# Three PSUM banks for each pair of a seven-product part, and other places for the weights of 256-column matmuls

## The chip, the cores and the metric

One core of one Trainium2 chip runs the program. The metric is the device time of one execution in microseconds, as the median over runs.

## The reference

A two-layer encoder trunk over 512 tokens of width 1024, in float32. Each layer adds four sub-layers to x: a SwiGLU of hidden width 2816, a mixer (retention and gated DeltaNet heads), a cross-attention to 256 memory rows, and a second SwiGLU. The change touches the SwiGLU most:

```python
def swiglu(u, w_gate, w_up, w_down):
    return (jax.nn.silu(u @ w_gate) * (u @ w_up)) @ w_down
...
for l in range(DEPTH):
    h = swiglu(rms_norm(x, norm_pre[l, 0]), ffn1_gate[l], ffn1_up[l], ffn1_down[l])
    x = x + 0.5 * rms_norm(h, norm_post[l, 0])
...
    h = swiglu(rms_norm(x, norm_pre[l, 3]), ffn2_gate[l], ffn2_up[l], ffn2_down[l])
    x = x + 0.5 * rms_norm(h, norm_post[l, 3])
```

## The kernel before, in words

**Two halves of every number.** TensorE works in a reduced float32. So every operand is held as a high part H and a rest L, and each product takes three matmuls, in this order: weights H with activations H, H with L, L with H (`mm3`, `mm3s`). In the trace such a matmul reads "out<-moving operand,weights". Three of them are called a triple below.

**The stream of weights.** `Stream` brings 1 MB raw tiles by DMA (two buffers, `raw`), and its thread `cutter` (line 431) cuts each into chunks: ScalarE writes H, VectorE writes L = raw - H. Chunks lie in one long tile `wts` (places of 2048 elements; `places`, line 379) or, around a change of sub-layer, in three extra pairs of tiles (`wHx`, `wLx`, made by `hl_tiles` in `transition`, line 817). `where` and `take` choose the place.

**Narrow and wide matmuls.** Most matmuls move 512 columns. 256 columns move in three places: the first group of each sub-layer (`first_group`, line 729, four chunks in two halves of the tokens), the K projection and the scores of the cross-attention, and the seven-product parts.

**Seven-product parts.** In `gate_up` (line 871) the gate and up columns from block `FAST` on are made 256 at a time. One such block of one of the two matrices is called a pair here (two 128-column stripes). It takes seven products of half size in place of eight (a Strassen scheme): each product is four triples, so a pair is 84 matmuls. `forms` (line 887) makes the sums S1 to S4 of the activations, S4 in place of A21; the cutter makes those of the weights, through the tile `T`. The four parts hold 3 + 9 + 9 + 9 blocks, which is 60 pairs and 5040 matmuls. A pair uses two PSUM banks of eight: Y (two partial sums side by side) and X. The order of the products in `stream` (line 961) and the waits between them are

```python
Y1 += c0 * A11;  Y0 += c1 * S1;  X0 += c0' * A12
yield lambda: r["a"]        # Y copied whole, 512 columns
Y0 += c3 * S4;   Y1 += c1' * S2;  X1 += c2 * A22
yield lambda: r["b"]        # Y1 copied, 256 columns
Y1 += c2' * S3
```

`post` (line 919) copies the intermediate sums to an SBUF tile `sg` on ScalarE (three copies), adds what is left in PSUM on VectorE (two of 512 columns), and takes Silu (gate) or multiplies by the gate into `h` (up, two of 512 columns).

**What sets the order.** The program is written out by a list scheduler (`Sched`, line 194): threads yield operations, and per engine the one that can start first by its cost table is emitted, with priorities. Each engine then runs its own queue in that order. `Banks` (line 318) hands out the eight PSUM banks, `Stream.prio` (line 468) sets how eager the cutter is by the number of chunks it is ahead.

**Where operands lie.** The allocator puts `wts` at byte 36,800 of each partition and `uH` at 196,544: 159,744 bytes apart, which is 624 x 256. `uL`, the S tiles and the extra tiles of the transitions behind a SwiGLU or a cross-attention are multiples of 256 away too. So a chunk at a place 2048 i begins at the same place of a 256-byte period as the operand that moves past it. Chunks of the seven-product parts are put 16 elements (64 bytes) on (`SHIFT`, line 366). In `mix` the tiles before the ring `hs` (seven of 128 bytes and one of 64, behind the 16 KB tile `oT`) end 64 bytes short of such a multiple, so the ring, and the extra tiles of the transition opened behind it, begin 64 bytes back.

Of the kernel before, what the change touches and what calls it, by code (L numbers as in the profile page):

```python
# [8 lines left out]
F32R = mybir.dt.float32r  # L9
# [3 lines left out]
ALU = mybir.AluOpType  # L13
AX = mybir.AxisListType

P = 128
D = 1024
S = 512
NT = S // P
KD = D // P  # L20
# [14 lines left out]
LEAD = 3  # L35

# [324 lines left out]
class Stream:  # L361
# [4 lines left out]
    SHIFT = 16  # L366

    def __init__(self, k):
        self.k = k
        self.raws, self.parts, self.loaded, self.chunks = [], [], {}, {}  # L370
        self.cut = self.taken = 0
        self.limit = self.slack = 0
        self.extra = []
        self.T = None

    def open(self, raw, w):
        self.rawring = Ring(raw)
        self.w, self.live = w, set()
        self.places = {"p": [(2048 * i, 1024) for i in range(HL_BUFS)],
                       "s": [(2048 * i + self.SHIFT, 1024) for i in range(HL_BUFS - 1)],  # L380
                       "h": [(2048 * (HL_BUFS - 1) + self.SHIFT, 512)]}

    def add(self, ap, a, b, kind):
# [3 lines left out]
    def cols(self, w, c0, kind="c"):  # L387
        self.add(w[:, c0:c0 + 256].rearrange("(k p) c -> p k c", p=P), KD, 256, kind)
# [18 lines left out]
    def where(self, c):  # L407

        if self.extra and c < self.limit:
            return self.extra  # L410
        i, j = self.parts[c]
        kind = "p" if self.raws[i][3] != "s" else "h" if j == 2 else "s"
        for pl in self.places[kind]:
            if all(pl[0] + 2 * pl[1] <= lo or lo + 2 * n <= pl[0] for lo, n in self.live):
                return kind, pl
        return None

    def take(self, c):
        ch, got = Chunk(), self.where(c)
        if got is self.extra:  # L420
            ch.home, ch.slot = got, got.pop(0)
            return ch, ch.slot
        kind, pl = got
        self.places[kind].remove(pl)
        self.places[kind].append(pl)
# [58 lines left out]
class Kernel:  # L484
# [26 lines left out]
    def hl_tiles(self, pool, i):  # L511
        return tuple(pool.tile([P, 1024], F32R, name=f"w{c}{i}") for c in "HL")

    def plan(self):

        A, st = self.D, self.st
        for l, i in self.subs:
            self.marks.append(len(st.parts))
            if i in (0, 3):
                g, u, d = (A[f"ffn{1 if i == 0 else 2}_{n}"][l] for n in ("gate", "up", "down"))  # L520
                for j in range(0, DFF, 256):
                    kind = "s" if (l, i) in FAST and j >= 256 * FAST[l, i] else "c"
                    st.cols(g, j, kind)
                    st.cols(u, j, kind)
                for k in range(0, DFF, 256):
                    st.rows(d, k)
            elif i == 1:
                w = A["w_in"][l]
                for c in (2560, 2048, 2816, 2304, 3072, 3328):
                    st.cols(w, c)  # L530
# [6 lines left out]
            else:  # L537
                q, k, v = (A[f"xattn_{n}"][l] for n in "qkv")
                for w, c in XORDER:
# [4 lines left out]
                    else:  # L544
                        st.cols(w, c)
# [271 lines left out]
    def transition(self, sub, nxt, stream, half=False, initial=False):  # L817

        n = 0 if initial else self.subs.index(sub) + 1
        with self.pool("trans") as tp:  # L820
# [9 lines left out]
            self.st.extra = [self.hl_tiles(tp, f"x{n}{i}") for i in range(HL_EXTRA)]  # L830
# [40 lines left out]
    def gate_up(self, h, made, ready, last, j0, nxt, hx):  # L871
# [8 lines left out]
        with self.pool("ffs") as fs:  # L880
# [38 lines left out]
            def post(r, j, up):  # L919
                o = yield from sg.get()  # L920
                yield lambda: r["n"] >= 2
                yield self.copy(o[:, 256:768], r["Y"].t)
                r["a"] = True
                yield lambda: r["n"] >= 5
                yield self.copy(o[:, 0:256], r["Y"].t[:, 256:])
                r["b"] = True
                yield lambda: r["n"] >= 7
                yield self.copy(o[:, 768:], r["Y"].t[:, 256:])
                r["c"] = True
                for b, sl in (("Y", slice(0, 512)), ("X", slice(512, 1024))):  # L930
                    yield V.tensor_tensor(out=o[:, sl], in0=r[b].t, in1=o[:, sl], op=ALU.add)
                    r[b].put()
# [6 lines left out]
                for q in (0, 1):  # L939
                    sl = slice(512 - 512 * q, 1024 - 512 * q)  # L940
                    yield self.mul(h[:, 2 * j + q], o[:, sl], g[:, sl])
                    ready.add(2 * j + q)
# [18 lines left out]
            def stream():  # L961
# [12 lines left out]
                for j in range(j0, KF // 2):  # L974
                    for up in range(2):
# [3 lines left out]
                        r = {"n": 0, "a": False, "b": False, "c": False}  # L979
                        r["Y"] = yield from self.banks.get(True)  # L980
                        r["X"] = yield from self.banks.get(True)
                        Y0, Y1 = r["Y"].t[:, :256], r["Y"].t[:, 256:]
                        X0, X1 = r["X"].t[:, :256], r["X"].t[:, 256:]
                        ths.append(sd.spawn(post(r, j, up), lambda r=r: 5 if r["c"] else -1, "post"))
# [12 lines left out]
                        st.free(c1)  # L997
# [3 lines left out]
                        yield lambda: r["b"]  # L1001
                        yield from product(r, Y1, half(c2, 1), S[2], last=True)
# [157 lines left out]
    def mix(self, l, nxt):  # L1160
# [6 lines left out]
        with self.pool("mix") as mp:  # L1167
# [20 lines left out]
            with self.pool("hs") as hp:  # L1188
                self.hring = [tuple(self.tile(hp, f"hs{c}{i}", [S], F32R) for c in "HL") for i in range(6)]
# [731 lines left out]
```

## Time and profile before

| | |
|---|---|
| median of 3 runs | 2445.86 us (2445.59 to 2447.47) |
| the profiled execution's own time | 2445.77 us |
| its span, first to last instruction | 2444.0 us |
| TensorE matmul busy | 2399.7 us (98%) |
| VectorE, ScalarE busy | 1686.7 us (69%), 1122.4 us (46%) |
| mean granted TensorE clock | 0.995 |
| chain that ended last | PE 19%, POOL 1%, the rest under 1% each |

The span is shorter than the time by 1.8 us, which lie before the first and after the last instruction. A matmul's row in a timeline has its start and a duration that overlaps the next one's (matmuls are pipelined); what one costs is the distance from start to start. All instructions stand under line 235, where the scheduler emits them, so groups are told apart by tile names.

### The profile page before, as it was taken

What the parts mean: (1) busy time and instruction counts of PE and PEld (TensorE: products, weight loads), DVE (VectorE), ACT (ScalarE), POOL (GpSimd) and SP (SyncE); (2) the same over time, 40 slices, a digit from 0 to 9 for tenths busy, and PEclk for the clock granted to TensorE, in tenths of its full rate; (3) what the DMA queues carried; (4) which work ended last, traced back from release to release, by engine and by line L of the source; (5) the groups of instructions that cost most, each with busy time, mean ns of one, the idle gap of its engine ahead of it and who ended that gap; (6) DMA issues with size and microseconds to landing.
All of it is one profiled execution on the core that took longest, in us unless ns stands there. A gap on an engine that the chain in (4) does not pass through costs nothing. (4 is left out here: it accounts for less than half of the span.)

```text
span 2444.0 us, 37654 instructions
## 1 busy us (share of the span) xinstructions
PE 2399.7 (98%) x15206; PEld 2128.4 (87%) x15206; DVE 1686.7 (69%) x2660; ACT 1122.4 (46%) x1886; POOL 203.4 (8%) x584
## 2 busy tenths in 40 slices
PE   8999999999999999999999999999999999999998
PEld 7889888886989889998889998888788898899987
DVE  5588637867776568886388885486877665788852
ACT  4524525742345544555245553366324454455631
POOL 1000001221020020001010000114010200100011
PEclk9999999999999999999999999999999999999999
DMA  6622522355334322334213334225553243133330
GB/s 204 202 95 82 177 86 96 99 175 159 99 121 153 109 86 70 114 108 176 86 35 104 106 120 160 81 93 145 163 153 132 89 164 104 35 104 104 127 141 35
DMA packets 231204, 286.83 MB, mean 117 GB/s; under 512 B 29630, under 2 KB 190966, under 8 KB 231030
## 3 DMA queue, kind: packets, MB, share of 16 engines
q1 hardware_dynamic: 229878, 280.23, 35.6%
q10 hardware_dynamic: 1152, 4.19, 0.4%
q8 instruction: 119, 1.95, 0.3%
q14 instruction: 55, 0.45, 0.1%
HBM read 255.00 MB, written 29.39 MB: 116 GB/s over the span
## 5 line engine op out<-in xcount | busy, mean ns | idle before, releaser
L235 PE MATMUL ps<-uH,wts 128*128 128x256 f32 (+1 forms) x4064 | 973.1, 325 | 2.5 <-ACT sg L235 2.0
L235 PEld LDWEIGHTS ps<-uH,wts 128*128 128x128 f32 x4064 | 690.3, 189 | 63.6 <-ACT sg L235 2.2
L235 PE MATMUL ps<-uL,wts 128*128 128x256 f32 (+1 forms) x2032 | 655.9, 323 | 0.6 <-DVE uL L235 0.6
L235 DVE TENSOR_TENSOR wts<-raw,wts 128x1024 fp32r<-128x1024 f32 (+1 forms) x363 | 408.5, 1134 | 141.9 <-ACT wts L235 139.3
L235 ACT ACTIVATE wts<-raw 128x1024 fp32r<-128x1024 f32 (+1 forms) x363 | 354.5, 983 | 202.8 <-PE ps L235 115.4
L235 PEld LDWEIGHTS ps<-uL,wts 128*128 128x128 f32 x2032 | 386.8, 190 | 30.8 <-DVE uL L235 1.5
L235 PE MATMUL ps<-wts,uH 128*128 128x512 f32 x1152 | 356.8, 391 | 0.0
L235 PEld LDWEIGHTS ps<-wts,uH 128*128 128x128 f32 x1152 | 214.9, 188 | 43.6
L235 PE MATMUL ps<-wts,uL 128*128 128x512 f32 x576 | 224.6, 390 | 0.0
L235 ACT ACTIVATE sg<-ps 128x256 f32<-128x256 f32 (+1 forms) x208 | 98.0, 473 | 273.1 <-PE ps L235 272.8
L235 DVE TENSOR_TENSOR wts<-T,wts 128x1024 fp32r<-128x1024 f32 x120 | 147.0, 1225 | 51.3 <-ACT wts L235 50.7
L235 ACT ACTIVATE wts<-T 128x1024 fp32r<-128x1024 f32 x120 | 126.9, 1057 | 62.8 <-DVE T L235 62.8
L235 PEld LDWEIGHTS ps<-wts,uL 128*128 128x128 f32 x576 | 108.2, 188 | 22.8
L235 DVE TENSOR_TENSOR uL<-h,uH 128x512 fp32r<-128x512 f32 x76 | 51.2, 689 | 107.5 <-ACT uH L235 107.4
L235 POOL TENSOR_SCALAR sm<-sm 128x1 f32<-128x1 f32 (+1 forms) x165 | 39.2, 238 | 836.8 <-ACT junk L235 812.1
L235 ACT ACTIVATE uH<-h 128x512 fp32r<-128x512 f32 x76 | 46.3, 626 | 132.0 <-PE ps L235 126.9
L235 ACT ACTIVATE junk<-ps 128x512 bf16<-128x512 f32 (+1 forms) x96 | 47.0, 490 | 113.6 <-PE ps L235 99.2
L235 POOL TENSOR_SCALAR wpost<-wpost 128x1024 f32<-128x1024 f32 x4 | 20.3, 5087 | 925.7 <-DMA wpost<-in_norm_post_dram 701.0
L235 PE MATMUL ps<-s3H,wts 128*128 128x256 f32 x480 | 94.6, 281 | 0.0
L235 PE MATMUL ps<-s2H,wts 128*128 128x256 f32 x480 | 94.6, 281 | 0.0
L235 PE MATMUL ps<-s1H,wts 128*128 128x256 f32 x480 | 94.6, 281 | 0.0
L235 DVE TENSOR_TENSOR sg<-ps,sg 128x512 f32<-128x512 f32 x120 | 79.9, 685 | 16.0 <-ACT sg L235 15.9
(340 smaller groups left out, 4324.4 us busy)
## 6 DMA issues: line engine op xcount, KB each, us to landing
raw<-in_ffn_up_dram SPq DMA_DIRECT2D x44, 1024.0 KB, 5.2
raw<-in_ffn_down_dram SPq DMA_DIRECT2D x44, 1024.0 KB, 4.9
raw<-in_ffn_gate_dram SPq DMA_DIRECT2D x43, 1024.0 KB, 5.2
raw<-in_w_in_dram SPq DMA_DIRECT2D x32, 1024.0 KB, 6.1
raw<-in_w_out_dram SPq DMA_DIRECT2D x8, 1024.0 KB, 5.7
raw<-in_xattn_q_dram SPq DMA_DIRECT2D x8, 1024.0 KB, 5.1
raw<-in_xattn_k_dram SPq DMA_DIRECT2D x8, 1024.0 KB, 5.0
raw<-in_xattn_v_dram SPq DMA_DIRECT2D x8, 1024.0 KB, 4.9
```

The lines of the kernel that those rows point to most:

```text
L235: fn(*a, **kw)
```

## The change

- `stream` takes three banks U, Y, X for a pair. U holds what was Y1, Y what was Y0. The product of S2 moves ahead of that of S4, so that between a sum and the product that goes on adding to its bank there are always two other products. `post` makes four copies of 256 columns (was 512, 256, 256) and three additions (256, 256, 512 columns, was two of 512).
- The two multiplications into `h` become one of 1024 columns.
- A shift is kept for each raw tile (`Stream.shifts`). Seven-product chunks lie 64 bytes on as before, but those of the first gate block of each part 60 bytes (15 elements). The chunks of each first group get 64 bytes if they land in an extra tile; in `wts` plain chunks stay unshifted. The extra tiles are now one tile of 2048 + 64 elements each, so that the shift fits.
- `mix` allocates a 64-byte tile `pad` ahead of the ring `hs`.

```diff
+NARROW = 16
...
-                       "s": [(2048 * i + self.SHIFT, 1024) for i in range(HL_BUFS - 1)],
-                       "h": [(2048 * (HL_BUFS - 1) + self.SHIFT, 512)]}
+                       "s": [(2048 * i, 1024) for i in range(HL_BUFS - 1)],
+                       "h": [(2048 * (HL_BUFS - 1), 512)]}
...
-        for pl in self.places[kind]:
+        for q in self.places[kind]:
+            pl = (q[0] + self.shifts[i] * (kind != "p"), q[1])
             if all(pl[0] + 2 * pl[1] <= lo or lo + 2 * n <= pl[0] for lo, n in self.live):
-                return kind, pl
+                return kind, q, pl
...
             ch.home, ch.slot = got, got.pop(0)
-            return ch, ch.slot
+            lo = self.shifts[self.parts[c][0]]
+            return ch, (ch.slot[:, lo:lo + 1024], ch.slot[:, lo + 1024:lo + 2048])
...
-                    kind = "s" if (l, i) in FAST and j >= 256 * FAST[l, i] else "c"
-                    st.cols(g, j, kind)
-                    st.cols(u, j, kind)
+                    fast = j - 256 * FAST[l, i]
+                    for w in (g, u):
+                        st.cols(w, j, "s" if fast >= 0 else "c",
+                                NARROW - 1 if fast == 0 and w is g else NARROW if fast >= 0 or j == 0 else 0)
...
-                    st.cols(w, c)
+                    st.cols(w, c, shift=NARROW if c in (2560, 2048) else 0)
...
-                        st.cols(w, c)
+                        st.cols(w, c, shift=NARROW if w is q and c < 512 else 0)
...
-            self.st.extra = [self.hl_tiles(tp, f"x{n}{i}") for i in range(HL_EXTRA)]
+            self.st.extra = [tp.tile([P, 2048 + 64], F32R, name=f"wx{n}{i}") for i in range(HL_EXTRA)]
...
-                yield lambda: r["n"] >= 2
-                yield self.copy(o[:, 256:768], r["Y"].t)
-                r["a"] = True
-                yield lambda: r["n"] >= 5
-                yield self.copy(o[:, 0:256], r["Y"].t[:, 256:])
-                r["b"] = True
-                yield lambda: r["n"] >= 7
-                yield self.copy(o[:, 768:], r["Y"].t[:, 256:])
-                r["c"] = True
-                for b, sl in (("Y", slice(0, 512)), ("X", slice(512, 1024))):
-                    yield V.tensor_tensor(out=o[:, sl], in0=r[b].t, in1=o[:, sl], op=ALU.add)
-                    r[b].put()
+                X, Y, U = r["X"], r["Y"], r["U"]
+                for n, sl, b in ((1, slice(0, 256), U), (2, slice(768, 1024), Y), (4, slice(512, 768), U), (7, slice(256, 512), U)):
+                    yield lambda: r["n"] >= n
+                    yield self.copy(o[:, sl], b.t[:, :256])
+                    r["c"] = n
+                for b, sl in ((Y, slice(512, 768)), (U, slice(768, 1024)), (X, slice(0, 512))):
+                    yield V.tensor_tensor(out=o[:, sl], in0=b.t[:, :sl.stop - sl.start], in1=o[:, sl], op=ALU.add)
+                    b.put()
...
-                for q in (0, 1):
-                    sl = slice(512 - 512 * q, 1024 - 512 * q)
-                    yield self.mul(h[:, 2 * j + q], o[:, sl], g[:, sl])
-                    ready.add(2 * j + q)
+                yield self.mul(h[:, 2 * j:2 * j + 2].rearrange("p a b -> p (a b)"), o, g)
+                ready.update((2 * j, 2 * j + 1))
...
-                        yield from product(r, Y1, half(c0, 0), A11, first=True)
+                        yield from product(r, U, half(c0, 0), A11, first=True)
                         c1 = yield from st.get()
                         yield lambda: formed[0]
-                        yield from product(r, Y0, half(c1, 0), S[0])
+                        yield from product(r, Y, half(c1, 0), S[0], first=True)
                         yield from product(r, X0, half(c0, 1), A12, first=True, last=True)
                         st.free(c0)
+                        yield lambda: r["c"] >= 1
+                        yield from product(r, U, half(c1, 1), S[1])
+                        st.free(c1)
                         c3 = yield from st.get()
-                        yield lambda: r["a"]
-                        yield from product(r, Y0, half(c3, 0), S4, last=True)
+                        yield lambda: r["c"] >= 2
+                        yield from product(r, Y, half(c3, 0), S4, last=True)
                         st.free(c3)
-                        yield from product(r, Y1, half(c1, 1), S[1])
-                        st.free(c1)
                         c2 = yield from st.get()
                         yield from product(r, X1, half(c2, 0), A22, first=True, last=True)
                         last[0] = end
-                        yield lambda: r["b"]
-                        yield from product(r, Y1, half(c2, 1), S[2], last=True)
+                        yield lambda: r["c"] >= 4
+                        yield from product(r, U, half(c2, 1), S[2], last=True)
                         st.free(c2)
...
             with self.pool("hs") as hp:
+                self.tile(hp, "pad", [NARROW])
                 self.hring = [tuple(self.tile(hp, f"hs{c}{i}", [S], F32R) for c in "HL") for i in range(6)]
```

## Rows read from the trace of the kernel before

**Rows 1.** The page: span, and busy time of the engines.
```profile
span 2444.0 us, 37654 instructions
PE 2399.7 (98%) x15206; PEld 2128.4 (87%) x15206; DVE 1686.7 (69%) x2660; ACT 1122.4 (46%) x1886; POOL 203.4 (8%) x584
```

**Rows 2.** Busy time in the four seven-product parts: length, PE, PEld, DVE, ACT, POOL, clock.
```profile
196.97:259.23 62.26, 59.76 (x505) 59.35 (x504) 53.32 (x62) 35.41 (x49) 0.00 (x0) 1.00 0.32 103
935.27:1113.35 178.08, 178.08 (x1514) 178.08 (x1512) 151.92 (x178) 96.84 (x137) 0.00 (x0) 1.00 0.34 108
1283.84:1461.92 178.08, 178.08 (x1514) 178.08 (x1513) 150.97 (x177) 96.49 (x136) 0.00 (x0) 1.00 0.34 110
2138.37:2316.47 178.10, 178.10 (x1513) 178.10 (x1512) 154.24 (x181) 97.39 (x137) 0.00 (x0) 1.00 0.34 108
```

**Rows 3.** Waits of PE over the whole span: us in total, times, longest.
```profile
PE ps L235 <- ACT sg L235: 2.0, 1, 2.0
```

**Rows 4.** Timeline of PE, first pair of the first part (start, duration, instruction).
```profile
198.56 0.28 PE L235 MATMUL ps<-uL,wts 128*128 128x256 f32 x1
...
199.24 0.28 PE L235 MATMUL ps<-s1L,wts 128*128 128x256 f32 x1
...
201.62 0.28 PE L235 MATMUL ps<-uL,wts 128*128 128x256 f32 x1
...
204.01 0.39 PE L235 MATMUL ps<-uH,wts 128*128 128x256 f32 x1 [2.00 <-ACT sg L235]
```

**Rows 5.** Timeline of ScalarE and VectorE before that wait ends.
```profile
201.47 1.06 ACT L235 ACTIVATE uH<-sg 128x1024 fp32r<-128x1024 f32 x1
...
203.38 0.58 ACT L235 ACTIVATE sg<-ps 128x512 f32<-128x512 f32 x1
...
202.56 1.23 DVE L235 TENSOR_TENSOR uL<-sg,uH 128x1024 fp32r<-128x1024 f32 x1
```

**Rows 6.** Timeline of PE, second pair of the first part.
```profile
214.12 0.28 PE L235 MATMUL ps<-uL,wts 128*128 128x256 f32 x1
...
215.18 0.28 PE L235 MATMUL ps<-uL,wts 128*128 128x256 f32 x1
```

**Rows 7.** Timeline of PE, first groups behind a cross-attention and behind the mixer.
```profile
903.16 0.28 PE L235 MATMUL ps<-uL,wHx 128*128 128x256 f32 x1
...
904.60 0.28 PE L235 MATMUL ps<-uL,wHx 128*128 128x256 f32 x1
...
738.14 0.28 PE L235 MATMUL ps<-uL,wHx 128*128 128x256 f32 x1
...
739.50 0.28 PE L235 MATMUL ps<-uL,wHx 128*128 128x256 f32 x1
```

**Rows 8.** Groups of PE by form: count, busy us, mean ns, idle before.
```profile
L235 PE MATMUL ps<-uH,wHx 128*128 128x256 f32 x208 | 60.1, 289 | 0.0
L235 PE MATMUL ps<-wts,hsH 128*128 128x512 f32 x192 | 60.0, 394 | 1.0 <-ACT hsH L235 1.0
```

**Rows 9.** Timeline of PE, output projections of the mixer and of a SwiGLU (512 columns).
```profile
689.94 0.39 PE L235 MATMUL ps<-wts,hsL 128*128 128x512 f32 x1
...
692.69 0.39 PE L235 MATMUL ps<-wts,hsL 128*128 128x512 f32 x1
...
299.83 0.39 PE L235 MATMUL ps<-wHx,uL 128*128 128x512 f32 x1
...
301.87 0.39 PE L235 MATMUL ps<-wHx,uL 128*128 128x512 f32 x1
```

**Rows 10.** Groups by form within the second part (935.3 to 1113.3): count, busy, mean ns.
```profile
L235 ACT ACTIVATE sg<-ps 128x256 f32<-128x256 f32 x35 | 13.4, 383 | 51.5 <-PE ps L235 51.5
L235 ACT ACTIVATE sg<-ps 128x512 f32<-128x512 f32 x18 | 10.7, 595 | 16.8 <-PE ps L235 16.8
...
L235 DVE TENSOR_TENSOR sg<-ps,sg 128x512 f32<-128x512 f32 x34 | 22.6, 685 | 2.6 <-ACT sg L235 2.6
...
L235 DVE TENSOR_TENSOR h<-sg,sg 128x512 f32<-128x512 f32 x16 | 10.6, 686 | 0.1
```

More of the change, by code (lines that the diff above doesn't have):

```diff
@@ L361 @@
 class Stream:
-    SHIFT = 16
     def __init__(self, k):
@@ L370, in __init__ @@
         self.raws, self.parts, self.loaded, self.chunks = [], [], {}, {}
+        self.shifts = []
         self.cut = self.taken = 0
@@ L379, in open, with add, cols @@
         self.places = {"p": [(2048 * i, 1024) for i in range(HL_BUFS)],
-                       "s": [(2048 * i + self.SHIFT, 1024) for i in range(HL_BUFS - 1)],
-                       "h": [(2048 * (HL_BUFS - 1) + self.SHIFT, 512)]}
-    def add(self, ap, a, b, kind):
+                       "s": [(2048 * i, 1024) for i in range(HL_BUFS - 1)],
+                       "h": [(2048 * (HL_BUFS - 1), 512)]}
+    def add(self, ap, a, b, kind, shift=0):
+        self.shifts.append(shift)
         self.parts += [(len(self.raws), j) for j in range(4 if kind == "s" else 2)]
         self.raws.append((ap, a, b, kind))
-    def cols(self, w, c0, kind="c"):
-        self.add(w[:, c0:c0 + 256].rearrange("(k p) c -> p k c", p=P), KD, 256, kind)
+    def cols(self, w, c0, kind="c", shift=0):
+        self.add(w[:, c0:c0 + 256].rearrange("(k p) c -> p k c", p=P), KD, 256, kind, shift)
     def block(self, w, r0, c0):
@@ L421, in take @@
             ch.home, ch.slot = got, got.pop(0)
-            return ch, ch.slot
-        kind, pl = got
-        self.places[kind].remove(pl)
-        self.places[kind].append(pl)
+            lo = self.shifts[self.parts[c][0]]
+            return ch, (ch.slot[:, lo:lo + 1024], ch.slot[:, lo + 1024:lo + 2048])
+        kind, q, pl = got
+        self.places[kind].remove(q)
+        self.places[kind].append(q)
         self.live.add(pl)
@@ L509, in __init__ @@
         self.xd = self.dr.tile([NT, P, D], F32, name="xd")
-    def hl_tiles(self, pool, i):
-        return tuple(pool.tile([P, 1024], F32R, name=f"w{c}{i}") for c in "HL")
     def plan(self):
@@ L978, in stream @@
                             begun = self.begin_splits(*out)
[L979 to L982, printed above, removed]
+                        r = {"n": 0, "c": 0}
+                        for b in "UYX":
+                            r[b] = yield from self.banks.get(True)
+                        Y, U = r["Y"].t[:, :256], r["U"].t[:, :256]
                         X0, X1 = r["X"].t[:, :256], r["X"].t[:, 256:]
-                        ths.append(sd.spawn(post(r, j, up), lambda r=r: 5 if r["c"] else -1, "post"))
+                        ths.append(sd.spawn(post(r, j, up), lambda r=r: 5 if r["c"] == 7 else -1, "post"))
                         c0 = yield from st.get()
-                        yield from product(r, Y1, half(c0, 0), A11, first=True)
+                        yield from product(r, U, half(c0, 0), A11, first=True)
                         c1 = yield from st.get()
                         yield lambda: formed[0]
-                        yield from product(r, Y0, half(c1, 0), S[0])
+                        yield from product(r, Y, half(c1, 0), S[0], first=True)
                         yield from product(r, X0, half(c0, 1), A12, first=True, last=True)
                         st.free(c0)
+                        yield lambda: r["c"] >= 1
+                        yield from product(r, U, half(c1, 1), S[1])
+                        st.free(c1)
                         c3 = yield from st.get()
-                        yield lambda: r["a"]
-                        yield from product(r, Y0, half(c3, 0), S4, last=True)
+                        yield lambda: r["c"] >= 2
+                        yield from product(r, Y, half(c3, 0), S4, last=True)
                         st.free(c3)
-                        yield from product(r, Y1, half(c1, 1), S[1])
-                        st.free(c1)
                         c2 = yield from st.get()
```

## The prediction

> **What bounds the kernel now.** I read the page first: TensorE is busy 98% of the span [rows 1], and the chain that ended last is mostly matmuls. So only what shortens TensorE's own time counts. Next the four seven-product parts, which the change rewrites: in the last three TensorE is busy for the whole stretch, 178.08 us of 178.08, at a clock of 1.00 (the 2.4 GHz level), while VectorE is busy for 85% and ScalarE for 54% [rows 2]. The list of TensorE's waits has a single one in all four parts for the copies that the change gives more room: 2.0 us, once [rows 3]. More room between a sum and its copy can therefore give back at most one stall of some 2 us directly.
>
> What is left is the pace. In the second part 1512 matmuls, which are 504 triples, take 178.08 us: **0.3533 us a triple** [rows 2], and 0.353 also in the first part (214.12 to 215.18 is three triples [rows 6]). But the first pair of the first part ran faster: 198.56 to 201.62 is nine triples in 3.06 us, **0.340 each**, at the same clock and with weights at the same 64 bytes on [rows 4]. It lasted through three products, until the one stall ended at 204.01 [rows 4], and never came back. A third pace stands in the first groups: unshifted extra tiles 0.360 (four triples, 903.16 to 904.60), and behind the mixer, where the extra tiles begin 64 bytes back, 0.340 (738.14 to 739.50) [rows 7]. Same shape, same clock, three paces. So the place of the weights against the moving operand sets the pace, and at 64 bytes on two paces are possible. Which of them a part falls into seems to be decided where it begins, and a stall can change it.
>
> Here a page disagrees. The Trainium skill ("TensorE: Matmul & The Clock Gate", Step-by-step: what each phase is for) says that the engine has two independent read ports, so that loading the next weights takes nothing from the running matmul. By that rule no placement would matter, and the sum below would keep only its stall; [rows 7] speak against it.
>
> **The change, part by part.**
>
> *The stall of the first part.* The product of S4 started at 204.01 [rows 4], where at pace it would have followed 201.62 by about two matmuls, at 201.85: 2.16 us lost. The copy that it waited for ended at 203.96 [rows 5]. In the new order the product of S2 comes first; its bank's copy is of the first sum, which has two products behind it, so it starts at 201.85 and fills 12 x 0.113 = 1.36 us, to 203.2. Then S4 needs its rest, `uL<-sg`, which ends at 203.79 [rows 5] and gets later by a 0.38 us copy [rows 10] if the copy of Y goes ahead of the cut at 201.47 [rows 5] on ScalarE. I take a stall of 0.8 in place of 2.16: **-1.4 us**, between 0 (the scheduler puts the cuts later) and -2.2.
>
> *Copies, additions, products into h.* Per pair ScalarE copies 4 x 0.383 = 1.53 us, was 0.595 + 2 x 0.383 = 1.36 [rows 10]: +0.17, hidden in the 46% that it idles. VectorE: one addition of 512 (0.685 [rows 10]) becomes two of 256, each between 0.34 (half) and 0.685; I take 0.41, since the 256-column copy too is 0.64 of the 512-column one [rows 10]; +0.14 a pair. Two products of 0.686 [rows 10] become one of 1024 columns, somewhere between one and two of these, near 1.23 as the 1024-column subtraction in [rows 5]: -0.14 per two pairs. Net +0.07 a pair, 1.2 us of VectorE in a part with 26 us of idle: 0. If the cover were gone it would cost 60 x 0.07 = 4 us.
>
> *Waits and queues.* Three waits on copies stand in a pair, was two. Behind each on TensorE is everything that follows, and the next pair. But each now has two products, 2.7 us, between the sum and the need, where one product, 1.35 us, has been enough in all pairs but one [rows 3]. Cost 0, above 0 only if a cut of 1.06 us stands wrongly twice in ScalarE's queue. The banks: two pairs in flight hold six of eight, and a pair's banks come back about 3 us after its last product, while the pair that needs them begins a pair (9.5 us) later. The down projection asks for four banks when at most three are still held. Cost 0. No DMA is added or moved; SP's and POOL's queues are as before.
>
> *The first tile 60 bytes on.* Four first gate blocks, 4 x 28 = 112 triples. No row shows 60 bytes. Bounds are the paces seen: 0.340 and 0.360, so -1.5 to +0.8 us; I take the 0.353 of its nearest place, 64: 0. Beside this its later neighbours overlap it by one element in the slot below, so the next block's second chunk may have to go elsewhere or wait for the pair's fourth product; it is needed a pair later, so 0.
>
> *Its effect on what follows.* This is the large term. If the part falls into the 0.340 pace and stays there, three parts gain 3 x 504 x 0.0133 = **-20.2 us**; the first, 156 more triples, another -2.1 if its smaller stall doesn't end the pace, which I leave out. If it stays at 0.353: 0. If it falls to 0.360: 1680 x 0.0067 = +11.3. I take the fast pace. For it: the same products at the same distance have run so [rows 4], the part's beginning is what the change alters, and the late copy that ended the pace then is what the change removes. Against it: the three later parts began without a wait and ran at 0.353 [rows 2], and no row shows that 60 bytes does better. At 0.340 a pair takes 9.52 us; VectorE's 151.92 / 18 + 0.07 = 8.5 us a pair [rows 2] still fits, with a ninth to spare, so the faster pace can be fed, though not by much.
>
> *First groups.* The extra tiles hold 624 of these matmuls (three groups of 208 [rows 8]): 528 of them, 176 triples, unshifted now, go from 0.360 to 0.353: -1.2. The 96 behind the mixer go from 64 bytes back to 64 on (`pad` moves them up, the shift again): 32 triples from 0.340 to 0.353, +0.4. Sum **-0.8**, between +0.4 (no gain) and -3.5 (176 triples at 0.340).
>
> *The pad.* The ring `hs` is the stationary side of 384 wide matmuls, 128 triples (192 of them in [rows 8]). They run at 0.6875 a triple (four in 2.75 us), against 0.680 in a SwiGLU's projection, where everything begins at one place (three in 2.04) [rows 9]. With the pad they lie as those do: 128 x 0.0075 = **-0.9**, between 0 and -0.9.
>
> The sum: -1.4 - 20.2 - 0.8 - 0.9 = -23.3 us. The profiled execution took 2445.77, of which 2444.0 is span, and stands 0.1 under the median of 2445.86. Forecast: **2422.5 us**.
>
> **The rivals.**
>
> *The pace stays* (0.353 in all parts). Then -1.4 - 0.8 - 0.9 = -3.1: 2442.7. For it: three of three parts that begun straight behind wide matmuls fell into this pace. Close to it lies the outcome by the skill's rule above, that placement counts for nothing: the stall alone, 2444.4. Both lie within 0.2% of before, 4.9 us, which is about what a measurement of this kernel can tell from no change. Chance 0.28 together.
>
> *The pace is won in some parts only.* A stall in a part ends it, as at 204.01 [rows 4], or VectorE with a ninth to spare falls behind. One part is worth 6.7 us: 2429 to 2440. Chance 0.16.
>
> *The pace gets worse.* The 60-byte tile starts the parts in the 0.360 pace, which this shape has at the place without a shift [rows 7], and the 64-byte tiles behind it keep it, as they keep whatever pace they are in over 1512 matmuls [rows 2]. Then +11.3 - 3.1 = +8.2: 2454. It decides from the second part's first pair on, and ends on the slower side if more than 28% of the 1680 triples are caught in it (3.1 us of gain are to be eaten up first). Chance 0.11.
>
> *The change doesn't do what it says* would be first-group chunks that no longer land in the extra tiles because these come free later: the 0.8 us are lost, no more. It is inside the first rival.
>
> **How the numbers follow.** Forecast 0.45, pace stays 0.28, some parts 0.16, worse 0.11. The likeliest alone reaches from 2417 (with the 2.1 us of the first part, and first groups at 0.340) to 2426. The range for 8 in 10 takes in the first two rivals: 2417 to 2446. Faster by over 0.2% (under 2441.0): forecast and partial wins, 0.61, and a little of the pace that stays where the stall and the first groups give their upper ends, 0.03: 0.64. Within 0.2%: 0.25. Slower by over 0.2%: 0.11.
>
> **What would show it.** In the profile after: the three later parts at 171.4 us, not 178.1; triples 0.340 apart in their timeline from the first pair to the last; no wait for `sg` over 1 us in the first part; 0.680 in the mixer's projection; first groups at 0.353 or less where the extra tiles are read. The forecast is wrong if the parts still last 178 us (the pace depends on something else than how a part begins), if they last 181 (the worse pace), or if new waits of TensorE for `wts` appear (VectorE has become the bound).

## The result, and the profile after

The changed kernel takes **2422.93 us** (median of 4 runs, 2422.38 to 2425.84) against 2445.73 (4 runs, 2443.38 to 2447.47) of the kernel before, run beside it: a ratio of 0.991, 95% interval 0.9893 to 0.9927. The forecast was 2422.5. The profiled execution is the longest of the four, 2425.84 us.

The page of the changed kernel, its first lines; TensorE's share of the span has not changed, its busy time has fallen by 20.7 us and the span by 20.0 [rows 1]:

```profile
span 2424.0 us, 37772 instructions
PE 2379.0 (98%) x15206; PEld 2107.0 (87%) x15206; DVE 1688.8 (70%) x2690; ACT 1134.3 (47%) x1946; POOL 194.7 (8%) x584
```

The four seven-product parts (stretch, its length, PE, PEld, DVE, ACT, POOL, clock, DMA share, GB/s), which answer to [rows 2]:

```profile
196.74:255.98 59.24, 58.18 (x506) 57.76 (x504) 52.42 (x64) 36.07 (x55) 0.00 (x0) 1.00 0.33 108
936.03:1107.94 171.91, 171.91 (x1514) 171.91 (x1513) 151.40 (x187) 100.50 (x155) 0.00 (x0) 1.00 0.34 111
1278.21:1450.12 171.91, 171.91 (x1514) 171.90 (x1512) 151.03 (x186) 99.88 (x154) 0.00 (x0) 1.00 0.34 111
2124.31:2296.21 171.90, 171.90 (x1514) 171.90 (x1512) 149.75 (x186) 100.65 (x154) 0.00 (x0) 1.00 0.34 111
```

The same matmuls at the same clock, with no idle time before or after in the long parts, are done 6.17, 6.17 and 6.20 us sooner; the first part gives 3.02. That is 21.6 us, nearly the whole result. Cut behind the first pair (84 matmuls), the second part shows where the pace changes:

```profile
936.03:946.07 10.04, 10.04 (x85) 10.04 (x84) 7.35 (x9) 4.75 (x7) 0.00 (x0) 1.00 0.34 106
946.07:1107.94 161.87, 161.87 (x1431) 161.87 (x1430) 144.05 (x179) 95.75 (x148) 0.00 (x0) 1.00 0.34 111
```

The 60-byte pair takes 10.04 / 84 = 119.5 ns a matmul, more than the 117.8 of the kernel before, and the 17 pairs behind it 161.87 / 1428 = 113.4. The timeline of TensorE at that border (start, duration, instruction):

```profile
945.47 0.29 PE L237 MATMUL ps<-s3L,wts 128*128 128x256 f32 x1
...
945.84 0.28 PE L237 MATMUL ps<-s3L,wts 128*128 128x256 f32 x1
...
946.54 0.28 PE L237 MATMUL ps<-uL,wts 128*128 128x256 f32 x1
946.65 0.39 PE L237 MATMUL ps<-uH,wts 128*128 128x256 f32 x2
946.88 0.28 PE L237 MATMUL ps<-uL,wts 128*128 128x256 f32 x1
```

In the last product at 60 bytes the pace is uneven, and the triple shown takes 0.37 us; in the first product at 64 a triple takes 0.34, and it does so to the part's end.

The list of TensorE's waits no longer has a line for `sg` [rows 3]. The line for `wts` has grown, from one wait to two, all in the first pair of the first part (before, then after):

```profile
PE ps L235 <- DVE wts L235: 0.5, 1, 0.5
```
```profile
PE ps L237 <- DVE wts L237: 1.1, 2, 0.6
```

The later of the two, the new one, on TensorE's timeline, and what VectorE did before it:

```profile
199.90 0.50 PE L237 MATMUL ps<-s1H,wts 128*128 128x256 f32 x2 [0.57 <-DVE wts L237]
```
```profile
197.50 1.22 DVE L237 TENSOR_TENSOR sg<-sg,uL 128x1024 f32<-128x1024 f32 x1
198.63 1.22 DVE L237 TENSOR_TENSOR wts<-T,wts 128x1024 fp32r<-128x1024 f32 x1
```

Outside the parts the two traces differ most in the mixers: the first is 4.0 us longer than before (408.17 to 721.91 became 404.77 to 722.50), the second 2.3 shorter. A stretch in the first mixer, after and then before (columns as above), shows most of why:

```profile
595.00:600.00 5.00, 5.00 (x56) 4.93 (x55) 1.94 (x3) 0.59 (x1) 2.57 (x3) 0.50 0.00 0
```
```profile
595.00:600.00 5.00, 5.00 (x120) 4.83 (x118) 3.38 (x5) 1.32 (x3) 2.88 (x3) 1.00 0.02 3
```

The granted clock was 0.50 (the 1.2 GHz level) in one and 1.00 (2.4) in the other, in a run of matmuls of 32 rows and 32 columns that both kernels have. Between the same two matmuls on either side of it, the first mixer lost 3.1 us here; another 1.4 it had lost around the wait for `k<-qkd` 20 to 30 us earlier. In the kernel before the clock fell so in the second mixer and not in the first. In the profiles of the experiments below it falls in one mixer, in both or in neither. Taken together the mixers are 1.7 us longer than before, 2.4 without what the pad gives there (experiment 8); that is most of the 2.8 us by which the spans differ less (20.0) than the medians (22.8).

### The profile page after: what moved, and what is told of

It is laid out like the page before. It is cut to its first block, busy times and chain, and to the rows that moved or that the text cites. A ratio compares the mean times of both kernels' runs of the same rounds, so it can differ in the third digit from the quotient of the medians.

```text
span 2424.0 us, 37772 instructions
## 1 busy us (share of the span) xinstructions
PE 2379.0 (98%) x15206; PEld 2107.0 (87%) x15206; DVE 1688.8 (70%) x2690; ACT 1134.3 (47%) x1946; POOL 194.7 (8%) x584
## 5 line engine op out<-in xcount | busy, mean ns | idle before, releaser
L237 PE MATMUL ps<-uH,wts 128*128 128x256 f32 (+1 forms) x4064 | 960.9, 322 | 0.5 <-DVE wts L237 0.5
L237 ACT ACTIVATE sg<-ps 128x256 f32<-128x256 f32 (+1 forms) x268 | 108.4, 406 | 257.9 <-PE ps L237 255.3
L237 PE MATMUL ps<-wx,uH 128*128 128x512 f32 x448 | 138.4, 390 | 0.0
L237 PEld LDWEIGHTS ps<-wts,uL 128*128 128x128 f32 x576 | 108.1, 188 | 22.6
L237 ACT ACTIVATE junk<-ps 128x512 bf16<-128x512 f32 (+1 forms) x96 | 47.0, 490 | 113.3 <-PE ps L237 99.2
L237 PEld LDWEIGHTS ps<-wx,uH 128*128 128x128 f32 x448 | 83.8, 188 | 17.2
```

Of the source, the lines that this page charges most:

```text
L237: fn(*a, **kw)
```

## The experiments

Times are medians, ratios are against the kernel before, run beside each. **Places** are bytes behind the start of a slot; by the addresses that the tiles were given, a slot's start and the moving operands are equal modulo 256 bytes. "Fast" is 113.3 ns a matmul (0.340 a triple), "slow" 117.8 (0.353).

**1. Without the 60-byte head.** The changed kernel with

```
-  NARROW - 1 if fast == 0 and w is g else NARROW if ...
+  NARROW if ...
```

> The changed kernel, with the first gate tile of each seven-product part 64 bytes on like all others. Theory (the 60-byte tile at the head of a part sets the pace that the 64-byte tiles behind it keep): the three long parts last 178.1 us again, triples 0.353 apart, and the time is 2423 + 3 x 6.2 = 2441.5, or 2443 with the first part slow too. Rival (the new order with three banks sets the pace): parts of 171.5, time 2422.

Measured: 2444.77 us, ratio 0.9999 (0.9989 to 1.0009). The second part:

```profile
934.23:1112.30 178.07, 178.07 (x1513) 178.06 (x1512) 150.33 (x186) 101.33 (x155) 0.00 (x0) 1.00 0.34 107
```

It took 178.08 and 178.07 in the other two. So the gain of the long parts hangs on one tile in each that lies four bytes lower than the rest. The first part needs no such tile. It was fast here, 58.56 us against 62.26 before: its first product waits 0.5 us for weights, and the matmuls behind that ran at 113.3, also behind a second wait of 0.4 us, for `sg`.

**2. The 60-byte head alone.** The kernel before, its banks and order as they were, with a shift kept for each raw tile as in the change, and

```
-  st.cols(g, j, kind)
+  st.cols(g, j, kind, 15 if j == 256 * FAST[l, i] else 16)
```

> The kernel before, two banks and old order, no other place changed, but the first gate tile of each part 60 bytes on. Theory (60-byte head): the long parts last 171.9 us, 0.340 a triple from the second pair on, time 2445.7 - 18.6 - 2.0 = 2425. Rival (order and banks): nothing moves, 2445.7. A third view (old order breaks the pace again and again by late copies): between, parts of 172 to 178.

Measured: 2439.38 us, 0.9976 (0.9965 to 0.9988). The second and the third part:

```profile
932.18:1110.33 178.15, 178.15 (x1513) 178.15 (x1512) 152.00 (x179) 96.29 (x136) 0.00 (x0) 1.00 0.34 108
1280.91:1453.13 172.22, 172.22 (x1513) 172.17 (x1512) 150.78 (x177) 96.38 (x136) 0.00 (x0) 1.00 0.36 113
```

The third part was fast to its end, and so were the first and the fourth (172.34); the second was fast for less than one pair. This execution is the shortest of the ten, 2433.86 us, and the longest took 2444.64. So in other executions more parts have probably lost the pace; none of them was traced. The timelines of TensorE and of ScalarE where it ended:

```profile
945.75 0.28 PE L235 MATMUL ps<-uL,wts 128*128 128x256 f32 x1
...
946.09 0.28 PE L235 MATMUL ps<-uL,wts 128*128 128x256 f32 x1
946.21 0.46 PE L235 MATMUL ps<-uH,wts 128*128 128x256 f32 x2
946.50 0.28 PE L235 MATMUL ps<-uL,wts 128*128 128x256 f32 x1
946.62 0.40 PE L235 MATMUL ps<-uH,wts 128*128 128x256 f32 x2
946.86 0.28 PE L235 MATMUL ps<-uL,wts 128*128 128x256 f32 x1
```
```profile
944.68 1.07 ACT L235 ACTIVATE wts<-T 128x1024 fp32r<-128x1024 f32 x1 [1.36 <-DVE T L235]
945.66 0.57 ACT L235 ACTIVATE sg<-ps 128x512 f32<-128x512 f32 x1
```

The triples start 0.34 apart, then once 0.41, then 0.36, and the rest of the part keeps 0.353. The late one, at 946.50, is the second matmul of the product of S4: it starts 0.19 us behind the first, which is the second of the two in the row of 946.21 and starts in time, at 946.32. The bank of that product is copied until 945.66 + 0.57 = 946.23, behind a cut of 1.07 us in ScalarE's queue. From this lateness of 0.07 us on, far too short to be in the list of waits, the pace was slow for the rest of the pair and the 16 behind it. That the close copy makes the start late is inferred: in the changed kernel, with two products between, none was late behind a part's first pair.

**3. The three banks alone.** The kernel before with the new order, copies and product into `h`, and the old places:

```
-  yield from product(r, Y0, half(c1, 0), S[0])
+  yield from product(r, Y, half(c1, 0), S[0], first=True)
...
+  yield lambda: r["c"] >= 1
+  yield from product(r, U, half(c1, 1), S[1])
```

> The kernel before with three banks, the new order and the one product into h alone; all places of tiles as before. Theory (60-byte head): only the stall of the first part shrinks, 2444.3, long parts of 178.1. Rival (order and banks set the pace): parts of 171.9, about 2425.

Measured: 2444.48 us, 0.9996 (0.9986 to 1.0005). The long parts took 178.08, 178.08 and 178.07. The first took 58.57 us, 3.7 less than before and 0.7 less than in the changed kernel: it began fast behind the same wait for weights as before, the wait for `sg` shrank from 2.0 us to 0.36, and the pace outlived it. So what the first part gains comes from the banks, not from the head; 3.7 us do not stand out in the time of a whole run.

**4. The places alone.** The changed kernel with two banks and the old order (the lines of experiment 3 the other way round).

> The changed kernel with two banks and the old order put back; all new places of tiles kept. Theory (60-byte head): long parts of 171.9; the stall of some 2 us in the first part returns, so 2424.5. Rival (order and banks): long parts of 178.1, about 2443.

Measured: 2440.32 us, 0.9985 (0.9975 to 0.9994). The third part, cut where its pace ended:

```profile
1281.63:1391.20 109.57, 109.57 (x962) 109.53 (x961) 95.11 (x112) 59.80 (x85) 0.00 (x0) 1.00 0.34 108
1391.20:1456.20 65.00, 65.00 (x553) 65.00 (x553) 55.77 (x66) 36.64 (x52) 0.00 (x0) 1.00 0.36 120
```

It was fast up to pair 11, and a late second matmul of the S4 product at 1391.30 (0.21 us behind the first) ended that. The second part fell in the pair behind its first (947.40), the fourth in pair 7 (2205.73, counted from 0); in the changed kernel, which differs only in banks, order and the one product into `h`, no start came late behind the first pair of a part. So the two halves of the change multiply: the banks alone give nothing that a time shows, the places alone 0.15%, both 0.9%. The head brings the pace, and the room behind the sums keeps it.

**5. All tiles at 60.** The changed kernel with

```
-  NARROW - 1 if fast == 0 and w is g else NARROW if fast >= 0 or j == 0 else 0
+  NARROW - 1 if fast >= 0 else NARROW if j == 0 else 0
```

> The changed kernel with every tile of the seven-product parts 60 bytes on, not the first alone. Theory (the 60-byte tile is only a way in: it runs unevenly itself, at some 118.4 ns a matmul, as the first pair of each part does in the changed kernel, and the 113.3 ns come with the 64-byte tiles behind it): the parts run at about 118 ns, 0.355 a triple, 178 to 179 us for each of the three long ones; 2443 to 2447 us, no change. Rival (60 bytes is itself a place of the fast pace, and the first pair is slow only because a part's beginning is slow anyway): 113.3 ns throughout, long parts at 171.4 to 172, about 2423.

Measured: 2454.67 us, 1.0051 (1.0035 to 1.0068). The third part:

```profile
1288.42:1469.10 180.68, 180.68 (x1513) 180.67 (x1512) 151.31 (x186) 99.70 (x154) 0.00 (x0) 1.00 0.32 106
```

That is 119.5 ns a matmul, the same as the head in the changed kernel, and never fast. (The 118.4 of the expectation came from a stretch that ended 0.09 us before the head's last matmul did.) The rival is out, and the theory's time missed by 8 us: as a place 60 is a bad one, and good only as a way in.

**6. All tiles at 192**, the place behind the mixer that was fast before [rows 7]:

```
-NARROW = 16
+NARROW = 48
...
-  NARROW - 1 if fast == 0 and w is g else NARROW if fast >= 0 or j == 0 else 0
+  NARROW if fast >= 0 or j == 0 else 0
...
-  self.tile(hp, "pad", [NARROW])
+  self.tile(hp, "pad", [16])
```

> The changed kernel with all shifted tiles 192 bytes on, the first one too, and the pad as it was. The place behind the mixer that ran at 0.340 in the kernel before was 64 bytes back, which is this place counted by 256. Theory (192 on is fast by itself and needs no head): all four parts at 113.3 ns from the first matmul, long parts 171.4 against 171.9, first groups with extra tiles at 0.340 and not 0.355: 4 x 0.4 + up to 2.5 us less than the changed kernel, 2419 to 2422. Rival (only a head that differs from its followers starts the fast pace, as with 60 before 64): long parts at 178 and 2441 to 2445. Second rival (the 0.340 behind the mixer hung on its short run, and in a long stream it breaks at late starts): parts between, 2429 to 2440.

Measured: 2442.69 us, 1.0004 (0.9995 to 1.0013). The long parts took 178.07, 178.08 and 178.08; the first, after the same wait as in experiment 1, was slow too. My theory fell for the parts: 192 isn't fast by itself. In the first groups behind a mixer or a cross-attention it was: the 24 matmuls of their second half that read an extra tile at 192, behind 12 at 0, ran at 113.3 ns, where the changed kernel, with 64 there, had 117.9.

**7. The head at 192**, the others at 64:

```
-  NARROW - 1 if fast == 0 and w is g else
+  48 if fast == 0 and w is g else
```

> The changed kernel with the first gate tile of each seven-product part 192 bytes on in place of 60, and the others 64 on as they are. Theory A (the tiles at 64 go on in whatever pace they are entered in): first tile at 113.3, the rest inherits it, long parts 171.4, 2420 to 2423. Theory B (it is the unevenness of the 60-byte tile that moves the matmuls against the loads into the fast rhythm, not the pace that it has): first tile 113.3, then 117.8, long parts 177.6 to 178, 2443 to 2445.

Measured: 2424.84 us, 0.9929 (0.9914 to 0.9944). The first pair of the second part and the pairs behind it, up to shortly before its end:

```profile
934.03:943.92 9.89, 9.89 (x86) 9.89 (x84) 7.14 (x7) 5.06 (x7) 0.00 (x0) 1.00 0.34 108
943.92:1098.00 154.08, 154.08 (x1362) 154.08 (x1361) 136.92 (x173) 90.54 (x140) 0.00 (x0) 1.00 0.34 110
```

Both theories were wrong in half. The head was slow (117.7), and the rest was fast all the same. So nothing is inherited, and an uneven head isn't needed: a *step* from another place onto 64 does it. Two parts lost 1.6 and 1.9 us in their last pair (TensorE, then ScalarE):

```profile
1101.85 0.39 PE L237 MATMUL ps<-s2H,wts 128*128 128x256 f32 x1 [1.35 <-ACT sg L237]
```
```profile
1100.47 1.06 ACT L237 ACTIVATE wts<-raw 128x1024 fp32r<-128x1024 f32 x1 [2.07 <-PE ps L237]
1101.43 0.64 ACT L237 ACTIVATE sg<-ps 128x256 f32<-128x256 f32 x2
```

A cut that waits 2.07 us for TensorE stands ahead of the copies in ScalarE's queue.

**8. Without the pad** (`self.tile(hp, "pad", [NARROW])` taken out).

> The changed kernel without the pad ahead of the mixer's ring. The forecast's term: 384 wide matmuls back from 0.680 to 0.6875 a triple, +0.9 us; the window of the mixer's output projection, 235 ns a matmul in the changed kernel, goes back to 237; and the first-group tiles behind the mixer lie 64 bytes further back, which may give 0 to -0.5 there. 2423 to 2424. Rival (the pad does nothing to the projection, whose 235 came from the SwiGLU before it): 235 stays, 2422.5 to 2423.

Measured: 2427.45 us, 0.9937 (0.9922 to 0.9952). The first mixer's output projection without the pad, and with it in the changed kernel:

```profile
673.01:710.00 36.99, 36.41 (x159) 29.18 (x158) 23.13 (x39) 18.10 (x32) 5.18 (x21) 1.00 0.56 199
```
```profile
674.67:711.33 36.66, 36.08 (x159) 29.16 (x158) 23.03 (x39) 18.10 (x32) 5.08 (x21) 1.00 0.57 201
```

The pad gives 0.33 us here and 0.34 in the second mixer; the kernel before took 36.99 here too. The rest of what this kernel takes more isn't in these stretches: its second mixer took 5.2 us longer than the changed kernel's, and ran at a granted clock of 0.84 and 0.82 for 20 us. A time can't tell 0.7 us from that, a stretch of the trace can.

**9. One odd tile in the middle.** All tiles at 64, but the gate tile of pair 8 of 18 at 192:

```
-  NARROW - 1 if fast == 0 and w is g else NARROW if ...
+  48 if w is g and j == (2304 if FAST[l, i] == 8 else 1536) else NARROW if ...
```

> The changed kernel with every tile of the seven-product parts 64 bytes on, the first one too, but for one gate tile in the middle, 192 on: pair 8 (counted from 0) of 18 in the long parts, pair 2 of 6 in the first. With all tiles at 64 the long parts took 177.96 us. Theory (what starts the fast pace is a step from one place to another while the matmuls stream, wherever it stands): pairs 0 to 8 at 117.8 ns a matmul, pairs 9 to 17 at 113.3, so 177.96 - 9 x 84 x 0.0044 = 174.6 for each long part, 10 us in all off the 2444.8 of all tiles at 64: 2433 to 2437. Rival, as the forecast had it (the beginning of a part decides its pace): 117.8 throughout, 178.0, 2443 to 2446.

Measured: 2437.28 us, 0.9978 (0.9968 to 0.9988). The third part, cut behind pair 8 (756 matmuls each):

```profile
1276.69:1365.75 89.06, 89.06 (x758) 89.05 (x757) 76.52 (x94) 48.50 (x75) 0.00 (x0) 1.00 0.34 107
1365.75:1451.40 85.65, 85.65 (x758) 85.65 (x757) 74.87 (x94) 51.28 (x79) 0.00 (x0) 1.00 0.35 112
```

117.8 ns up to the odd tile, and through it, and 113.3 from the first matmul of the next: 174.7 us, as the theory of the step had it. The beginning of a part isn't needed. Nor is a disturbance: the starts around that border lie 0.113 to 0.119 us apart, none of them late. The other two long parts changed at the same pair and gave 1.7 us back in their last one, as in experiment 7.

**10. The mirror.** First tile at 64, the others at 192:

```
-  NARROW - 1 if fast == 0 and w is g else NARROW if fast >= 0 or j == 0 else 0
+  NARROW if fast == 0 and w is g or fast < 0 and j == 0 else 48 if fast >= 0 else 0
```

> The changed kernel the other way round: the first gate tile of each seven-product part 64 bytes on, the others 192. All at 192 took 177.96 us in the long parts, all at 64 the same, 192 ahead of 64 was fast. Theory (any step between places starts the fast pace): 113.3 ns a matmul from pair 1 on, long parts 171.6 to 172, 2421 to 2425. Rival (the fast pace belongs to 64 on, and 192 can't run so in a long stream): 117.8 throughout, 178.0, 2441 to 2446.

Measured: 2443.33 us, 1.0001 (0.9992 to 1.0011); the long parts took 178.08, 178.07 and 178.07. A step from 64 onto 192 does nothing in the parts. Yet 192 can be fast in a long stream: the first part, which begins with a wait of 0.5 us for weights, was fast from there to its end:

```profile
197.49:256.05 58.56, 57.70 (x505) 57.29 (x504) 52.42 (x64) 36.09 (x55) 0.00 (x0) 1.00 0.33 109
```

**11. The first groups moved too.** The shift of 64 also for the first groups' tiles in the common ring and for the K projection:

```
-  pl = (q[0] + self.shifts[i] * (kind != "p"), q[1])
+  pl = (q[0] + self.shifts[i], q[1])
...
-  wp.tile([P, HL_BUFS * 2048], F32R, name="wts")
+  wp.tile([P, HL_BUFS * 2048 + NARROW], F32R, name="wts")
...
-  st.cols(w, c, shift=NARROW if w is q and c < 512 else 0)
+  st.cols(w, c, shift=0 if w is q and c >= 512 else NARROW)
```

> The changed kernel with the 64 bytes given to all weight tiles of the first groups, the ones in the common ring too and not only the extra ones, and to the tiles of the K projection. They run at 120 ns a matmul unshifted. Theory (the place is all that matters): 912 and 384 matmuls at 117.8 in place of 120, 1296 x 0.0022 = -2.9 us: 2419 to 2421; at 113.3, where a group's start brings that pace, up to -8.7: 2414. Rival (a shifted tile reaches 64 bytes into the next slot of the ring, whose tile then can't be cut ahead, and TensorE waits for weights behind the first groups): the gain is eaten, 2422 to 2428, with new waits of TensorE for weights at the wide matmuls.

Measured: 2490.01 us, 1.0192 (1.0174 to 1.021). The time says little on the question. The longest line of TensorE's waits:

```profile
PE ps L237 <- DVE tmp L237: 54.2, 10, 8.7
```

That is 36 us more than the changed kernel's 18.1, at the changes of sub-layer, and not the waits for weights that the rival named. And the ring, 64 bytes longer, pushed the tiles allocated behind it 64 bytes on, by their addresses: the S tiles, the extra tiles and the K projection's moving operand, but not `uH` and `uL`. So the stretches do say something. The first groups' tiles in the ring now lay at 64 against `u`, and in six of the eight longer stretches of them (48 to 71 matmuls) they took 113.6 to 113.8 ns, in the other two 115.8 and 117.8. The K projection's weights and moving operand both moved, and stayed at 120. In the parts the weights lie at 64 against `u` and at 0 against the S tiles, and the pace changes with the product (second part):

```profile
1000.18 0.28 PE L237 MATMUL ps<-s2L,wts 128*128 128x256 f32 x1
...
1000.54 0.28 PE L237 MATMUL ps<-s2L,wts 128*128 128x256 f32 x1
...
1001.61 0.28 PE L237 MATMUL ps<-uL,wts 128*128 128x256 f32 x1
...
1001.95 0.28 PE L237 MATMUL ps<-uL,wts 128*128 128x256 f32 x1
```

A triple takes 0.36 against S2 and 0.34 against `u`, with the weights at one place; the part's mean of 116.2 ns is a mixture of the two. This is the one run that shows that the place counts against the moving operand and not by itself. The down projection behind the second part rose from 226.7 to 228.8 ns a matmul. Why `tmp` comes later was not traced.

**12. Three other trials, one in each long part**: all tiles at 128 in the second, only the first *chunk* at 60 in the third, all at 32 in the fourth:

```
+  32 if (l, i) == (0, 3) else 8 if (l, i) == (1, 3) else NARROW if fast or w is u else
+  (NARROW - 1, NARROW) if (l, i) == (1, 0) else NARROW - 1
```

> The changed kernel with another trial in each of three of its seven-product parts; the first part is as in the changed kernel. Second part: all tiles 128 bytes on, no head. Theory (what counts is the distance from the place of the moving operand, 64 and 192 being the same distance on two sides and 0 the worst): 128, the farthest, runs at 113.3 ns without a head, 171.3 us for the part; rival (128 is one more place with two paces, or as slow as 0): 177.96 to 181.3. Third part: only the first of the four chunks of the first gate tile 60 bytes on, the rest 64. Theory (the step alone matters, and the 60-byte head is itself the slow stretch): fast within the first pair, 171.4 to 171.7 against 171.9; rival (a short head doesn't do it): 177.96. Fourth part: all tiles 32 bytes on, no head. Theory (between 0 with 120 ns and 64 with 117.8): 178 to 181.3; rival (32 is a fast place): 171.4. By the theories the time is 0.5 + 0.4 less and 6 to 9.4 more than the changed kernel, 2428 to 2432; by the rivals it lies between 2422 and 2445.

Measured: 2445.65 us, 1.0008 (0.9997 to 1.0018). The three parts:

```profile
931.20:1112.64 181.44, 181.44 (x1513) 181.44 (x1512) 150.51 (x187) 101.36 (x155) 0.00 (x0) 1.00 0.32 105
1282.94:1454.47 171.53, 171.53 (x1513) 171.53 (x1512) 151.35 (x187) 99.87 (x154) 0.00 (x0) 1.00 0.34 111
2132.57:2315.45 182.88, 180.50 (x1513) 179.28 (x1512) 151.96 (x186) 99.17 (x154) 0.00 (x0) 1.00 0.33 105
```

128 is as slow as 0 (120.0 ns), 32 lies at 118.3 beside its three stalls, and neither is fast. The short head is enough: the second product, at 64, was fast from its third matmul on, the third, at 60 again, slow, and the fourth fast. This part is the shortest of all: 171.53. In all four parts it would save some 0.4 us each, 0.06% of the time, under what a measurement of this kernel can tell; it wasn't run as a kernel of its own.

## Why the prediction was right, point by point

- **The effect on what follows, -20.2: right in size, and the mechanism as far as "two paces at one place".** The three parts gave 18.5. What is missing are the first pairs, which stayed slow in each part: 3 x (10.04 - 9.52) = 1.6. That a head at 60 bytes would bring the fast pace was a choice without a row, as the prediction says; that it came true was in part luck, for the reason given beside it failed, as the next point says.
- **"Which of them a part falls into seems to be decided where it begins"** is the step that failed. Experiment 9 puts the odd tile in the middle of a part, and the pace changes there. In the long parts of these runs a step of the weights from 60 or 192 onto 64 while the matmuls stream brought it; the part's first tile is only where the change put it.
- **"The late copy that ended the pace then is what the change removes"** held, more sharply than written. The prediction took the 2.0 us stall for what ended it. In experiments 2 and 4 the pace ended at starts that were late by 0.07 to 0.1 us, so the claim that one product between sum and need "has been enough in all pairs but one" was true of the list of waits and not of the starts. This is why the room of three banks, which alone shows in no time (experiment 3), is worth some 18 us with the head.
- **The first tile 60 bytes on, 0 between -1.5 and +0.8:** 10.04 us a pair against 9.89, four pairs, +0.6 us.
- **The stall of the first part, -1.4:** measured -1.4 too, but by other stalls. TensorE waited 2.0 us for `sg` and 0.5 for weights; now it waits 0.5 and 0.57 us for weights and not for `sg`. The new wait is for the second chunk, whose subtraction VectorE did behind `sg<-sg,uL`. The part's other 1.6 us are the pace, which the sum had left out (-2.1): five pairs gained 1.8, and the first, at 60 bytes, lost 0.2.
- **Copies, additions and products, 0:** the busy times held. Within the second part of the changed kernel the new forms (count, busy us, mean ns) are

```profile
L237 DVE TENSOR_TENSOR sg<-ps,sg 128x256 f32<-128x256 f32 x34 | 13.4, 418 | 0.7
L237 DVE TENSOR_TENSOR sg<-ps,sg 128x512 f32<-128x512 f32 x17 | 11.6, 681 | 0.0
L237 DVE TENSOR_TENSOR h<-sg,sg 128x1024 f32<-128x1024 f32 x8 | 9.8, 1219 | 0.0
```

  against estimates of 0.41 and 1.23 from [rows 10] and [rows 5]. VectorE had the ninth to spare that the fast pace needs.
- **Waits and queues, 0:** held in the changed kernel. Experiments 7 and 9 show the condition that the prediction named, a cut standing wrongly in ScalarE's queue: 1.6 to 1.9 us where it happens.
- **First groups, -0.8:** -0.8 in the runs of matmuls themselves, over the seven changes of sub-layer, but what lies between those runs took longer, and from the first start to the last only -0.3 is left. The second half of both groups behind the mixer lost 0.1, where the prediction had +0.4 in all; one of them took 12.98 us where it took 12.87.
- **The pad, -0.9:** -0.7 (experiment 8).

Together, -21.6 in the parts, -0.3 and -0.7 make -22.6, and the medians differ by 22.8; that the profiled spans show less, 20.0, is mostly the mixers' clock.

Of the rivals, *the pace stays* is what the long parts of experiments 1, 3, 6 and 10 do, *won in some parts only* is experiments 2 and 4, and *the pace gets worse* is experiment 5: each was a neighbour of the change, one tile's place or one bank away. The rule of the Trainium skill ("TensorE: Matmul & The Clock Gate", Step-by-step: what each phase is for), two independent read ports, taken as the prediction took it, would have given one pace in all these runs. Between 113.3 and 120.0 ns, with nothing changed but the weights' place, the measurement decides against that reading; whether it is the reads that collide, no run here shows.

## What to carry to other kernels

Where an engine is busy all the time, look at the distance from start to start of equal instructions, not at the waits: 3.5% of TensorE's time in the long parts (178.08 us against 171.91) stood in no list. A pace that has two values at one setting has to be both brought about and protected, and two changes that give nothing or little alone can be most of the gain together, so test the pair as well as the parts. And a tile made a few bytes longer moves those that are allocated behind it; keep its size, or compare every pace again.

## What was not expected of the hardware

- The pace of a 256-column fp32r matmul by the place of its weights, counted from the moving operand's by 256 bytes, all at a granted clock of 1.00:

| place | ns a matmul | where |
|---|---|---|
| 0 | 120.0 | first groups, K projection; experiment 11 |
| 32 | 118.3 | experiment 12 |
| 60 | 119.5, uneven | heads, experiment 5 |
| 64 | 117.8 or 113.3 | experiments 1 and 9 |
| 128 | 120.0 | experiment 12 |
| 192 | 117.8 or 113.3 | [rows 7]; experiments 6 and 10 |

- At 64 and 192 the pace depends on what went before. In the parts a step onto 64 from 60 or 192 brings the fast one; from 64 onto 192 doesn't, nor does a start behind 512-column matmuls. In the first groups 24 matmuls at 192 behind 12 at 0 were fast (experiment 6), 24 at 64 behind 12 at 0 weren't (117.9, changed kernel), and in experiment 11 the pace came with the moving operand. So the steps listed here are not yet a rule. A wait of half a microsecond for weights in the first product brought the fast pace where that product's tile lay at 64 (the kernel before, experiments 1, 3, 9 and 10) and not where it lay at 192 (6 and 7); once there, it outlasted a step onto 192 (10).
- In the profiles of experiments 2 and 4, 15 starts behind the first pairs came 0.07 to 0.1 us late, all of them the second matmul of the S4 product. At five the fast pace ended, as at 946.50 in experiment 2 and at 1391.30 in experiment 4; at ten it did not, as at 1353.10 in the same part of experiment 4. Which ones do, and what in the engine holds the two rhythms apart, these runs leave open.
